# A macaron block with retention and pooling: the inverse roots of the norms go to all partitions by a store to DRAM and a broadcast load instead of by products with diagonal matrices

## The chip, the core and the metric

The kernel runs on one core of one Trainium2 chip. The time is that of the device for one execution, in microseconds, as the median over several executions. The profiled execution is one more of the same program, taken by the hardware profiler; its span runs from its first instruction to its last.

## What is computed

The reference takes x of 1024 tokens by 1024 channels in float32 and runs one layer (cut to what matters):

```python
h = h + 0.5 * swiglu_ffn(rmsnorm(h, norm_ffn1), ffn1_w_in, ffn1_w_out)      # D_FF = 2816
u = rmsnorm(h, norm_mix)
q, k, v, g_ret, p, gates = split(u @ w_in)                                    # 7168 columns
q, k = rotary(q), rotary(k) * 256 ** -0.5                                     # 4 heads of 256
ret = retention(q, k, v)                                                      # chunks of 64, decayed state
ret = ret * rsqrt(mean(ret * ret) + 1e-6) * silu(g_ret)
pool_out = multiscale_pool(p, pool_w, pool_scale)                             # windows 2, 4, 8, 16
merged = sigmoid(gate_0) * (ret @ w_ret_up) + sigmoid(gate_1) * (pool_out @ w_pool_up)
h = h + merged @ w_out
h = h + 0.5 * swiglu_ffn(rmsnorm(h, norm_ffn2), ffn2_w_in, ffn2_w_out)
out = rmsnorm(h, norm_final)
# rmsnorm(x, g) = x * rsqrt(mean(x * x) + 1e-6) * g, over the channels of each token
```

There are four RMS norms: n1 ahead of the first feed-forward part, n2 ahead of the mixing part, n3 ahead of the second feed-forward part, and the final one.

## The kernel before

Activations lie with channels on the 128 partitions and tokens along the free dimension: a tile of 128 by 1024 holds 128 channels of all tokens, a half of it (`half(t, j)`) 512 tokens. Each float32 operand of a product is split into a rounded part (a cast on ScalarE, line 141) and the rest (a subtraction on VectorE, line 142), and each product is three TensorE passes (lines 161 to 163). The large products go by a Strassen-like scheme of seven block products (`strassen`); a group's products are named by their weights, L11, S2, S1, S3, L12, S4, L22, and its banks a, b and e. `ffn_in` computes gate and up of a feed-forward part in 22 groups of 128 columns (`a0`, `a11`, `a1`, ... in the first, `c0`, `c11`, `c1`, ... in the second), `ffn_out` the way back (names with `b` and `d`), `projections` the products of the mixing part.

A norm's factor depends on the token alone, so it is not applied to the operand: the gain per channel goes into the operands, and the factor multiplies the results as they leave PSUM or later. For that the factor must stand on every partition as a row of 1024 numbers, the tile `rb` (`n1rb`, `n2rb`, `n3rb`). `inverse_root` (lines 184 to 207) yields a tile `r` with tokens on the partitions: 128 by 8 for a norm, 128 by 4 or 128 by 2 for a part of the last norm. `token_sums` gets there by products with a column of ones. `spread` (lines 217 to 225) turns `r` into rows: for each group of 128 tokens VectorE multiplies the identity matrix by a column of r (line 223), and one product of a matrix of ones with these diagonals (line 224) puts the row on every partition in a PSUM bank. `Next.stats` does that twice for 512 tokens each and copies both halves to `rb` on ScalarE (line 321).

The final norm comes in three parts of tokens as the last products end (`Last.end`): part 0 is tokens 512 to 1023, part 1 tokens 0 to 255, part 2 tokens 256 to 511. The last product of `ffn_out` is cut the same way: `near` computes the left 256 columns of the four banks `dp6b0` to `dp6b3` for all eleven steps, `far(i)` then the right 256 columns of one bank after the other. As each ends, `part` adds it to the residual (line 721: an eviction `dacc<-dp6b`), squares are summed into `n4ssq` (lines 242 and 243), and when all four are in, the part's sum (`fin0sum`, `fin1sum`, `fin2sum`, line 213), root, factor (`fin0b`, `fin1b`, `fin2b`) and eight scalings (line 1284) follow, each with a store to the output.

All DMAs are issued by SP (`load`, line 129), in one queue, in an order that a scheduler sets with the orders of the other engines when the program is built; instructions of one engine run in that order. A transfer that has to wait holds those behind it. Where a factor's tile exists already when an eviction is written, `ffn_in` uses it there (line 489); otherwise it multiplies later (line 493). Background work is handed out between products by `Flow`; `tc.high_priority` marks evictions.

Of the kernel before, what the change touches and what calls it, by code (L numbers as in the profile page):

```python
# [10 lines left out]
F32 = mybir.dt.float32  # L11
# [6 lines left out]
P = 128  # L18
# [66 lines left out]
def block_kernel(ctx: ExitStack, tc, x, x_tok, vecs, f1_in, f1_out, w_in, pool_w, w_ret, w_pool, w_o,  # L85
                 f2_in, f2_out, rope, decay, consts, out):
    nc = tc.nc
# [4 lines left out]
    copy = nc.scalar.copy  # L92
# [6 lines left out]
    dr = ctx.enter_context(tc.tile_pool(name="dr", bufs=1, space=bass.MemoryType.DRAM))  # L99
# [9 lines left out]
    def raw(name):  # L109
        return sb.tile([P, S], F32, tag="raw", bufs=N_RAW, name=name)  # L110
# [4 lines left out]
    def t4(name):  # L115
        return sb.tile([P, S], F32, tag="t4", bufs=N_T4, name=name)

    def c2(name):
        return sb.tile([P, H], F32, tag="c2", bufs=N_C2, name=name)

    def bank(name):
        return ps.tile([P, H], F32, tag="ps", name=name)
# [5 lines left out]
    def load(dst, src):  # L128
        nc.sync.dma_start(dst, src)
# [4 lines left out]
    def half(t, j):  # L134
        return t[:, j * H : (j + 1) * H]
# [48 lines left out]
    def inverse_root(sums, n, name, by=None):  # L184

        m = sums.shape[-1]

        def st(k):
            return sb.tile([P, 8], F32, tag="st", bufs=10, name=f"{name}{k}")[:, :m]

        v, r0, r1, t = st("v"), st("r0"), st("r1"), st("t")
        if by is None:
            nc.vector.tensor_scalar(v, sums, 1.0 / n, EPS, MUL, ADD)
        else:
            tt(v, sums, by[0], MUL)
            nc.vector.tensor_scalar(v, v, EPS, None, ADD)
        act(r0, v, AF.Sqrt)
        nc.vector.reciprocal(r1, r0)

        tt(t, r1, r1, MUL)  # L200
        tt(t, t, v, MUL)
        nc.vector.tensor_scalar(t, t, -0.5, 1.5, MUL, ADD)
        r = sb.tile([P, 8], F32, tag="rt", bufs=3, name=f"{name}r")[:, :m]
        tt(r, r1, t, MUL)
        if by is not None:
            tt(r, r, by[1], MUL)
        return r

    def token_sums(ssq, tiles, name):

        sums = bank(f"{name}sum")
        for k, j in enumerate(tiles):
            mm(sums[:, k : k + 1], ssq[:, j * P : (j + 1) * P], ones[:, :1], start=k == 0, stop=True,
               skip_group_check=True)
        return sums[:, : len(tiles)]

    def spread(r, name):

        n = r.shape[-1]
        b = bank(f"{name}b")[:, : n * P]  # L220
        dg = c2(f"{name}dg")[:, : n * P]
        for j in range(n):
            nc.vector.tensor_scalar(dg[:, j * P : (j + 1) * P], ident, r[:, j : j + 1], None, MUL)
        mm(b, ones, dg, start=True, stop=True)
        return b

    class Norm:


# [15 lines left out]
    class Next(Norm):  # L245
# [69 lines left out]
        def stats(self, sums=None):  # L315
            def go():
                r = inverse_root(sums if sums is not None else token_sums(self.ssq, range(8), self.name), D, self.name)
                self.r_tok = r
                rb = t4(f"{self.name}rb")
                for q in range(2):  # L320
                    copy(half(rb, q), spread(r[:, 4 * q : 4 * q + 4], f"{self.name}{q}"))
                self.rb = rb

            flow.add(go)
# [434 lines left out]
    ra, rb = raw("ra"), raw("rb")  # L759
# [506 lines left out]
    class Last(Norm):  # L1266
# [6 lines left out]
        def end(self, part):  # L1273
            tokens = (slice(H, S), slice(0, HD), slice(HD, H))[part]
            at = {}

            def stats():
                r = inverse_root(token_sums(self.ssq, range(tokens.start // P, tokens.stop // P), f"fin{part}"), D,
                                 f"fin{part}")
                at["b"] = spread(r, f"fin{part}")  # L1280

            def scale(mt):
                t = self.tiles[mt][:, tokens]
                stt(t, t, vec[:, V_FINAL + mt : V_FINAL + mt + 1], at["b"], MUL, MUL)
                load(out[mt, :, tokens], t)

            flow.add(stats, *(lambda mt=mt: scale(mt) for mt in range(KT)))

    fin = Last("n4")
# [92 lines left out]
```

## Time and profile before

| | |
|---|---|
| median of 3 runs | 2199.36 us (2199.76, 2199.36, 2197.19) |
| profiled execution | 2200.49 us |
| its span | 2198.7 us, 27345 instructions |
| TensorE busy | 2179.3 us, 99% |
| VectorE busy | 1628.7 us, 74% |
| ScalarE busy | 966.6 us, 44% |
| DMA queue of SP | 109152 packets, 308.05 MB, 40.0% of 16 engines' span |
| granted TensorE clock, mean | 0.998 |

Names: PE is the TensorE product and PEld its weight load, DVE is VectorE, ACT is ScalarE, SPq the sequencer of SP that issues the DMAs. A row of a timeline has start and length in us, engine, line, operation, written tile, read tiles, shapes, and in brackets how long the engine was idle before and what ended that. A matmul with float32 operands is recorded as two (x2). In the chain of waits a row is the piece of the span that the chain spends in that work. `x16, 128.0 KB, 1.8` in the list of DMA issues means sixteen transfers of 128 KB, a median of 1.8 us from issue to landing.

### The profile page before, as it was taken

The page shows a single profiled execution, that of the slowest core. Times are in us where ns is not written, and L with a number is a line of the kernel's source. Part 1 is how long each engine was busy: PE and PEld are TensorE (multiplying, and loading weights), DVE is VectorE, ACT ScalarE, POOL GpSimd, SP SyncE. Part 2 cuts the span into 40 slices and gives each one's busy share as a digit, 9 for nine tenths or more (in the row PEclk, how much of TensorE's full clock was granted, in tenths as well). Part 3 has the DMA queues.
Part 4 walks back from the last instruction along what each step waited for, and adds up shares of the span by engine and source line. Part 5 has one row for each costly group of instructions (what it writes and reads, how often), then busy time and mean ns, then how long its engine had stood idle before and what let it go on. Part 6 is the DMA issues. An engine that isn't in the chain of part 4 may idle for free.

```text
span 2198.7 us, 27345 instructions
## 1 busy us (share of the span) xinstructions
PE 2179.3 (99%) x10108; PEld 1818.6 (83%) x10108; DVE 1628.7 (74%) x2682; ACT 966.6 (44%) x1702; POOL 0.2 (0%) x4
## 2 busy tenths in 40 slices
PE   9999999999999999999999999999999999999998
PEld 7888888888888888888888998888888888888887
DVE  8787677887686777686867667775877777788775
ACT  7533333444554434334346554443533333344451
POOL 0000000000000000000000000000000000000000
PEclk9999999999999999999999999999999999999999
DMA  5244232495323323233235465363142323249522
GB/s 210 96 152 150 91 119 97 149 327 185 129 93 119 133 101 128 103 115 115 103 127 201 146 214 202 125 220 125 58 144 101 125 92 114 98 153 331 183 85 77
DMA packets 109287, 309.80 MB, mean 141 GB/s; under 512 B 12257, under 2 KB 14433, under 8 KB 109153
## 3 DMA queue, kind: packets, MB, share of 16 engines
q1 hardware_dynamic: 109152, 308.05, 40.0%
q8 instruction: 79, 1.29, 0.2%
q14 instruction: 56, 0.45, 0.1%
HBM read 218.35 MB, written 89.65 MB: 140 GB/s over the span
## 4 chain that ended last, share of the span: by engine, by line
PE 92%; DVE 3%; DMA 3%; ACT 1%; issue 1%; SPq 0%; DVEq 0%; ACTq 0%
PE c_b L161 3%; PE c_b L163 3%; PE c_b L162 3%; PE a_b L161 2%; PE a_b L162 2%; PE a_b L163 2%; PE c_a L161 2%; PE c_e L163 2%; PE c_a L163 2%; PE c_e L162 2%; PE c_e L161 2%; PE c_a L162 2%; PE a_e L162 2%; PE a_e L163 2%; PE a_e L161 2%; PE a_a L162 2%
## 5 line engine op out<-in xcount | busy, mean ns | idle before, releaser
L141 ACT CAST c_wS<-c_S 128x512 fp32r<-128x512 f32 x88 | 54.7, 622 | 132.3 <-PE c_b L163 76.5
L141 ACT CAST a_wS<-a_S 128x512 fp32r<-128x512 f32 x84 | 52.3, 622 | 106.7 <-PE a_b L163 71.6
L142 DVE TENSOR_TENSOR c_wS<-c_S,c_wS 128x512 fp32r<-128x512 f32 x88 | 60.8, 691 | 24.8 <-ACT c_wS L141 24.2
L142 DVE TENSOR_TENSOR a_wS<-a_S,a_wS 128x512 fp32r<-128x512 f32 x84 | 58.0, 690 | 23.7 <-ACT a_wS L141 23.3
L161 PE MATMUL c_a<-n3R,c_wL 128*128 128x512 f32 x176 | 68.6, 390 | 0.0
L162 PE MATMUL c_b<-n3T,c_wS 128*128 128x512 f32 x176 | 68.5, 389 | 0.0
L161 PE MATMUL c_b<-n3T,c_wS 128*128 128x512 f32 x176 | 68.5, 389 | 0.0
L162 PE MATMUL c_a<-n3R,c_wL 128*128 128x512 f32 x176 | 68.5, 389 | 0.0
L163 PE MATMUL c_a<-n3R,c_wL 128*128 128x512 f32 x176 | 68.5, 389 | 0.0
L163 PE MATMUL c_b<-n3T,c_wS 128*128 128x512 f32 x176 | 68.5, 389 | 0.0
L161 PE MATMUL a_a<-n1R,a_wL 128*128 128x512 f32 x168 | 65.8, 391 | 0.0
L163 PE MATMUL a_a<-n1R,a_wL 128*128 128x512 f32 x168 | 65.4, 389 | 0.0
L162 PE MATMUL a_a<-n1R,a_wL 128*128 128x512 f32 x168 | 65.4, 389 | 0.0
L161 PE MATMUL a_b<-n1T,a_wS 128*128 128x512 f32 x168 | 65.4, 389 | 0.0
L162 PE MATMUL a_b<-n1T,a_wS 128*128 128x512 f32 x168 | 65.4, 389 | 0.0
L163 PE MATMUL a_b<-n1T,a_wS 128*128 128x512 f32 x168 | 65.4, 389 | 0.0
L141 ACT CAST c_wL<-c_ra 128x512 fp32r<-128x512 f32 x44 | 27.3, 621 | 43.4 <-PE c_e L163 38.0
L141 ACT CAST a_wL<-a_ra 128x512 fp32r<-128x512 f32 x42 | 26.0, 621 | 38.0 <-PE a_e L163 38.0
L142 DVE TENSOR_TENSOR c_wL<-c_ra,c_wL 128x512 fp32r<-128x512 f32 x44 | 30.4, 691 | 11.7 <-ACT c_wL L141 11.4
L162 PEld LDWEIGHTS c_b<-n3T,c_wS 128*128 128x128 f32 x176 | 33.0, 188 | 6.9
L162 PEld LDWEIGHTS c_a<-n3R,c_wL 128*128 128x128 f32 x176 | 33.0, 188 | 6.9
L163 PEld LDWEIGHTS c_a<-n3R,c_wL 128*128 128x128 f32 x176 | 33.0, 188 | 6.9
(2369 smaller groups left out, 7225.7 us busy)
## 6 DMA issues: line engine op xcount, KB each, us to landing
c_ra<-in_f_in SPq DMA_DIRECT2D x22, 512.0 KB, 3.6
c_rb<-in_f_in SPq DMA_DIRECT2D x22, 512.0 KB, 5.1
a_ra<-in_f_in SPq DMA_DIRECT2D x21, 512.0 KB, 3.6
a_rb<-in_f_in SPq DMA_DIRECT2D x21, 512.0 KB, 5.2
t<-au SPq DMA_DIRECT2D x11, 512.0 KB, 2.7
b<-an SPq DMA_DIRECT2D x11, 512.0 KB, 3.2
r<-au SPq DMA_DIRECT2D x11, 512.0 KB, 3.8
br<-r SPq DMA_DIRECT2D x11, 512.0 KB, 6.0
```

Source lines behind the costliest of these rows:

```text
L141: copy(hi, src)
L142: tt(lo, src, hi.bitcast(F32), SUB)
L161: mm(dst, w[0], m[0], start=start, stop=False, skip_group_check=True)
L162: mm(dst, w[0], m[1], start=False, stop=False, skip_group_check=True)
L163: mm(dst, w[1], m[0], start=False, stop=stop, skip_group_check=True)
```

## The change

A new function `spread_by_dma` writes the tile r to a line in DRAM, one number per token, and loads that line back to all 128 partitions. The line's store has runs of one number (128 by 8 by 1 for a norm); the load reads the same 4 KB (2 KB for part 0 of the final norm, 1 KB for part 1) once for each partition. The three norms load into `rb`; parts 0 and 1 of the final norm load into a tile in SBUF instead of the PSUM bank. Part 2 of the final norm keeps `spread`.

```diff
--- before.py
+++ after.py
@@ -224,6 +224,14 @@
         mm(b, ones, dg, start=True, stop=True)
         return b
 
+    def spread_by_dma(r, name, dst):
+
+        n = r.shape[-1]
+        line = dr.tile([n, P], F32, tag=f"{name}line", name=f"{name}line")
+        with nc.allow_non_contiguous_dma(reason="one number per token"):
+            load(line.rearrange("j p -> p j"), r)
+        load(dst, line.rearrange("j p -> (j p)").unsqueeze(0).to_broadcast([P, n * P]))
+
     class Norm:
 
 
@@ -317,8 +325,7 @@
                 r = inverse_root(sums if sums is not None else token_sums(self.ssq, range(8), self.name), D, self.name)
                 self.r_tok = r
                 rb = t4(f"{self.name}rb")
-                for q in range(2):
-                    copy(half(rb, q), spread(r[:, 4 * q : 4 * q + 4], f"{self.name}{q}"))
+                spread_by_dma(r, self.name, rb)
                 self.rb = rb
 
             flow.add(go)
@@ -1277,7 +1284,11 @@
             def stats():
                 r = inverse_root(token_sums(self.ssq, range(tokens.start // P, tokens.stop // P), f"fin{part}"), D,
                                  f"fin{part}")
-                at["b"] = spread(r, f"fin{part}")
+                if part == 2:
+                    at["b"] = spread(r, f"fin{part}")
+                else:
+                    at["b"] = c2(f"fin{part}b")[:, : tokens.stop - tokens.start]
+                    spread_by_dma(r, f"fin{part}", at["b"])
 
             def scale(mt):
                 t = self.tiles[mt][:, tokens]
```

On SP's queue each pair stands as line and load: behind n1's line come the two weight loads of group a13, then the load; behind n2's line its load directly, ahead of the stores of v0 and v1; n3's line stands behind group c12's first weight load, the second one comes between line and load; fin0's pair stands ahead of all stores to the output, fin1's between part 0's stores and part 1's. On TensorE fin1sum moves behind 8 products of far(1).

The scheduler also places other work differently; the prediction speaks of three places. VectorE in the third norm, before, from the first use of the factor on (`c0_a` to `c11_b` are PSUM banks of the first two groups of the second feed-forward part, `c1_...` weights of the third):

```order
L489 TENSOR_TENSOR cg0_13283<-c0_a_13117,n3rb_13307 128x512
L489 TENSOR_TENSOR cg11_13344<-c11_a_13155,n3rb_13307 128x512
L489 TENSOR_TENSOR cg0_13283<-c0_b_13149,n3rb_13307 128x512
L142 TENSOR_TENSOR c1_wL11_13401<-c1_ra_13397,c1_wL11_13401 128x512
L142 TENSOR_TENSOR c1_wS3_13433<-c1_S3_13431,c1_wS3_13433 128x512
L489 TENSOR_TENSOR cg11_13344<-c11_b_13168,n3rb_13307 128x512
L347 TENSOR_TENSOR c1_S1_13457<-c1_rb_13398 128x512
L493 TENSOR_TENSOR cu11_13345<-cu11_13345,n3rb_13307 128x512
L347 TENSOR_TENSOR c1_S2_13459<-c1_S1_13457,c1_ra_13397 128x512
L487 TENSOR_TENSOR cu0_13284<-c0_e_13264,c0_v_13193 128x512
L502 TENSOR_TENSOR cu0_13284<-cg0_13283,cu0_13284 128x512
L142 TENSOR_TENSOR c1_wS2_13461<-c1_S2_13459,c1_wS2_13461 128x512
```

Now, beginning with the ninth instruction behind the root n3r:

```order
L142 TENSOR_TENSOR c1_wL11_13362<-c1_ra_13358,c1_wL11_13362 128x512
L142 TENSOR_TENSOR n3T42_13411<-h2_6_12925,n3T42_13411 128x512
L142 TENSOR_TENSOR n3T43_13415<-h2_7_13081,n3T43_13415 128x512
L354 TENSOR_TENSOR c1_S2_13420<-c1_S1_13418,c1_ra_13358 128x512
L142 TENSOR_TENSOR c1_wS3_13394<-c1_S3_13392,c1_wS3_13394 128x512
L496 TENSOR_TENSOR cg0_13257<-c0_a_13091,n3rb_13281 128x512
L496 TENSOR_TENSOR cg0_13257<-c0_b_13123,n3rb_13281 128x512
L496 TENSOR_TENSOR cg11_13305<-c11_a_13129,n3rb_13281 128x512
L496 TENSOR_TENSOR cg11_13305<-c11_b_13142,n3rb_13281 128x512
L142 TENSOR_TENSOR c1_wS2_13422<-c1_S2_13420,c1_wS2_13422 128x512
L500 TENSOR_TENSOR cu0_13258<-cu0_13258,n3rb_13281 128x512
```

The four multiplications by n3rb stand behind the split of the weights c1_wS3 and together ahead of that of c1_wS2; before, wS3 stood between them.

VectorE at the end, part 0 of the final norm, before (from its fifth scaling on):

```order
L1284 SCALAR_TENSOR_TENSOR dacc4_16559<-dacc4_16559,vec_66,fin0b_17926 128x512
L1284 SCALAR_TENSOR_TENSOR dacc5_16561<-dacc5_16561,vec_66,fin0b_17926 128x512
L1284 SCALAR_TENSOR_TENSOR dacc6_16563<-dacc6_16563,vec_66,fin0b_17926 128x512
L1284 SCALAR_TENSOR_TENSOR dacc7_16565<-dacc7_16565,vec_66,fin0b_17926 128x512
L721 SCALAR_TENSOR_TENSOR dacc4_16559<-dp6b0_16391,dacc4_16559 128x256
L721 SCALAR_TENSOR_TENSOR dacc5_16561<-dp6b1_16392,dacc5_16561 128x256
L721 SCALAR_TENSOR_TENSOR dacc6_16563<-dp6b2_16393,dacc6_16563 128x256
L721 SCALAR_TENSOR_TENSOR dacc7_16565<-dp6b3_16394,dacc7_16565 128x256
L243 TENSOR_TENSOR n4ssq_17340<-n4ssq_17340,n4q4_0_18117 128x256
L243 TENSOR_TENSOR n4ssq_17340<-n4ssq_17340,n4q5_0_18120 128x256
L243 TENSOR_TENSOR n4ssq_17340<-n4ssq_17340,n4q6_0_18123 128x256
```

Now:

```order
L1295 SCALAR_TENSOR_TENSOR dacc4_16520<-dacc4_16520,vec_66,fin0b_17887 128x512
L728 SCALAR_TENSOR_TENSOR dacc4_16520<-dp6b0_16352,dacc4_16520 128x256
L728 SCALAR_TENSOR_TENSOR dacc5_16522<-dp6b1_16353,dacc5_16522 128x256
L728 SCALAR_TENSOR_TENSOR dacc6_16524<-dp6b2_16354,dacc6_16524 128x256
L728 SCALAR_TENSOR_TENSOR dacc7_16526<-dp6b3_16355,dacc7_16526 128x256
L1295 SCALAR_TENSOR_TENSOR dacc5_16522<-dacc5_16522,vec_66,fin0b_17887 128x512
L1295 SCALAR_TENSOR_TENSOR dacc6_16524<-dacc6_16524,vec_66,fin0b_17887 128x512
L1295 SCALAR_TENSOR_TENSOR dacc7_16526<-dacc7_16526,vec_66,fin0b_17887 128x512
L251 TENSOR_TENSOR n4ssq_17301<-n4ssq_17301,n4q4_0_18075 128x256
L251 TENSOR_TENSOR n4ssq_17301<-n4ssq_17301,n4q5_0_18078 128x256
L251 TENSOR_TENSOR n4ssq_17301<-n4ssq_17301,n4q6_0_18081 128x256
```

Three of the eight scalings by fin0b stand behind the four evictions of near's banks; five stand ahead of them.

VectorE at the end, part 1, before:

```order
L1284 SCALAR_TENSOR_TENSOR dacc0_16551<-dacc0_16551,vec_66,fin1b_18144 128x256
L1284 SCALAR_TENSOR_TENSOR dacc1_16553<-dacc1_16553,vec_66,fin1b_18144 128x256
L1284 SCALAR_TENSOR_TENSOR dacc2_16555<-dacc2_16555,vec_66,fin1b_18144 128x256
L1284 SCALAR_TENSOR_TENSOR dacc3_16557<-dacc3_16557,vec_66,fin1b_18144 128x256
L721 SCALAR_TENSOR_TENSOR dacc5_16561<-dp6b1_16392,dacc5_16561 128x256
L1284 SCALAR_TENSOR_TENSOR dacc4_16559<-dacc4_16559,vec_66,fin1b_18144 128x256
L1284 SCALAR_TENSOR_TENSOR dacc5_16561<-dacc5_16561,vec_66,fin1b_18144 128x256
L1284 SCALAR_TENSOR_TENSOR dacc6_16563<-dacc6_16563,vec_66,fin1b_18144 128x256
L1284 SCALAR_TENSOR_TENSOR dacc7_16565<-dacc7_16565,vec_66,fin1b_18144 128x256
L243 TENSOR_TENSOR n4ssq_17340<-n4ssq_17340,n4q5_256_18236 128x256
L721 SCALAR_TENSOR_TENSOR dacc6_16563<-dp6b2_16393,dacc6_16563 128x256
L243 TENSOR_TENSOR n4ssq_17340<-n4ssq_17340,n4q6_256_18239 128x256
```

Now:

```order
L1295 SCALAR_TENSOR_TENSOR dacc0_16512<-dacc0_16512,vec_66,fin1b_18102 128x256
L1295 SCALAR_TENSOR_TENSOR dacc1_16514<-dacc1_16514,vec_66,fin1b_18102 128x256
L1295 SCALAR_TENSOR_TENSOR dacc2_16516<-dacc2_16516,vec_66,fin1b_18102 128x256
L1295 SCALAR_TENSOR_TENSOR dacc3_16518<-dacc3_16518,vec_66,fin1b_18102 128x256
L728 SCALAR_TENSOR_TENSOR dacc6_16524<-dp6b2_16354,dacc6_16524 128x256
L1295 SCALAR_TENSOR_TENSOR dacc4_16520<-dacc4_16520,vec_66,fin1b_18102 128x256
L1295 SCALAR_TENSOR_TENSOR dacc5_16522<-dacc5_16522,vec_66,fin1b_18102 128x256
L1295 SCALAR_TENSOR_TENSOR dacc6_16524<-dacc6_16524,vec_66,fin1b_18102 128x256
L1295 SCALAR_TENSOR_TENSOR dacc7_16526<-dacc7_16526,vec_66,fin1b_18102 128x256
L251 TENSOR_TENSOR n4ssq_17301<-n4ssq_17301,n4q6_256_18196 128x256
L728 SCALAR_TENSOR_TENSOR dacc7_16526<-dp6b3_16355,dacc7_16526 128x256
L251 TENSOR_TENSOR n4ssq_17301<-n4ssq_17301,n4q7_256_18233 128x256
```

The eviction of far(1), dp6b1, stands ahead of the scalings by fin1b, and those of far(2) and far(3), dp6b2 and dp6b3, behind four and eight of them.

## The prediction, made before the changed kernel had run

> **What bounds the kernel now.** I read the page first: busy time by engine, and the chain that ended last.
>
> ```profile
> span 2198.7 us, 27345 instructions
> PE 2179.3 (99%) x10108; PEld 1818.6 (83%) x10108; DVE 1628.7 (74%) x2682; ACT 966.6 (44%) x1702; POOL 0.2 (0%) x4
> ...
> PE 92%; DVE 3%; DMA 3%; ACT 1%; issue 1%; SPq 0%; DVEq 0%; ACTq 0%
> ```
>
> TensorE is busy for all but 19 us and is 92% of the chain. Then I asked for busy time in the stretches around three of the places that change (columns: stretch, its length, then busy us and count of PE, PEld, DVE, ACT, POOL, then clock and DMA):
>
> ```profile
> 80.00:100.00 20.00, 20.00 (x86) 15.88 (x85) 15.35 (x32) 10.88 (x17) 0.00 (x0) 1.00 0.12 41
> 1560.00:1600.00 40.00, 40.00 (x181) 32.47 (x180) 36.72 (x70) 22.47 (x38) 0.00 (x0) 1.00 0.26 77
> 2157.00:2187.00 30.00, 29.69 (x241) 28.95 (x240) 17.58 (x49) 3.05 (x9) 0.00 (x0) 1.00 0.29 106
> ```
>
> In all three TensorE has no room: 20.00 of 20.00, 40.00 of 40.00, 29.69 of 30.00 us. Whatever leaves its queue moves the end forward by as much, unless something new makes it wait. VectorE (36.72 of 40) has little room around the third norm. So two questions decide: what do the removed products cost TensorE, and does a factor that now comes by DMA arrive before somebody on TensorE's path needs it?
>
> **What is removed.** The chain of waits, in order of time, has the products that go (start, length, what):
>
> ```profile
> 88.52 0.86 PE n10b L224 x2
> 89.38 0.86 PE n11b L224 x2
> ...
> 674.65 1.12 PE n20b L224 x2
> 675.77 0.86 PE n21b L224 x2
> ...
> 1577.37 0.86 PE n30b L224 x2
> 1578.23 0.86 PE n31b L224 x2
> ...
> 2161.35 0.86 PE fin0b L224 x2
> ...
> 2176.67 0.43 PE fin1b L224 x2
> ```
>
> First norm 0.86 + 0.86 = 1.72, second 1.12 + 0.86 = 1.98 (0.26 of it a wait for its diagonal), third 1.72: 5.42 us. fin0 0.86, fin1 0.43. **Together 6.71 us off the path.** The diagonals on VectorE and ScalarE's six copies into the rb tiles go too; I cost them at nothing, because TensorE covers them in the rows above; without that cover they would be a further gain, not a loss.
>
> **What is added.** Five pairs of DMAs on SP's queue: a store of n numbers per partition, one number per run, and a load of the line to all 128 partitions; SP waits between them. No such store is in the trace. The nearest rows: a store and a load of the same tensor one behind the other (SP's timeline, then the landing times of these two), single transfers by size from the list of issues, the landing of the 128x64 vector load, and all packets of the queue:
>
> ```profile
> 127.38 0.32 SPq L129 DMA_DIRECT2D r<-au  x1
> ...
> 130.04 0.32 SPq L129 DMA_DIRECT2D br<-r  x1
> ...
> DMA to landing us min/median/max: 2.6/2.9/3.2
> ...
> out<-dacc SPq DMA_DIRECT2D x16, 128.0 KB, 1.8
> dec<-in_decay SPq DMA_DIRECT2D x4, 256.0 KB, 3.2
> c_rb<-in_f_in SPq DMA_DIRECT2D x22, 512.0 KB, 5.1
> ...
> DMA to landing us min/median/max: 1.9/1.9/1.9
> ...
> q1 hardware_dynamic: 109152, 308.05, 40.0%
> ```
>
> The pair of 512 KB transfers takes 2.6 (store landed; the load goes out 2.66 after it) + 3.2 = 5.9 us. That is the template. The open term is p, the time of one 4-byte element on its DMA engine. With 16 engines there are 64 elements per engine for a norm (1024 numbers), 32 for fin0, 16 for fin1. Below, p is 0: then the store is no slower than the smallest one, 1.8 us. Above, p is that of an average packet of 2.8 KB: 0.400 x 2198.7 x 16 / 109152 = 129 ns. I take **p = 40 ns**, nearer to nothing: from 128 to 512 KB the rows go from 1.8 to 2.6 us, so time there follows bytes, and an element has 4. Loads: 1.9 (the small vector) to 3.2 us; 3.2 for fin0 (256 KB, as dec), 2.5 between the two for fin1 (128 KB), 5.1 for the norms, whose load goes out among weight loads. SP's turn adds 0.1 (2.66 against 2.6). So from root to factor: fin0 1.8 + 1.3 + 3.2 + 0.1 = 6.4 us (4.4, with a load of 2.5, to 9.2), fin1 1.8 + 0.6 + 2.5 + 0.1 = 5.0 (4.0 to 7.2).
>
> The Trainium skill's page "DMA: Bandwidth & Descriptors", in its section on the anatomy of one DMA, gives a fit of 2.0 us plus bytes over 436 GB/s (for DMAs that GpSimd issues; these come from SP): an estimate from it is 4.6 us for fin0 and 4.3 for fin1, and the sum by that would be the full 6.7.
>
> **Where the factor is needed.** VectorE's timeline: when each root is done and what stands at or just ahead of its first use; then SP's first transfer behind the new pair of the second norm, and TensorE's product that bounds the third norm:
>
> ```profile
> 74.03 0.17 DVE L204 TENSOR_TENSOR n1r<-n1r,n1t 128x8 f32<-128x8 f32 x1
> 86.54 0.69 DVE L142 TENSOR_TENSOR a_wL<-a_ra,a_wL 128x512 fp32r<-128x512 f32 x1
> ...
> 671.37 0.17 DVE L204 TENSOR_TENSOR n2r<-n2r,n2t 128x8 f32<-128x8 f32 x1
> 696.19 0.69 DVE L841 TENSOR_TENSOR p0A<-p0a,n2rb 128x512 f32<-128x512 f32 x1 [0.29 <-PE p0a L163]
> ...
> 1575.22 0.16 DVE L204 TENSOR_TENSOR n3r<-n3r,n3t 128x8 f32<-128x8 f32 x1
> ...
> 677.89 0.33 SPq L129 DMA_DIRECT2D v<-v0A  x1
> ...
> 1597.34 0.39 PE L161 MATMUL c_b<-n3T,c_wS 128*128 128x512 f32 x1
> ```
>
> Norm 1: the first use stands behind the a_wL split, 13 us after the root. Norm 2: 24 us. Norm 3: in the new order 13 VectorE instructions of 0.6 to 0.7 us stand ahead of it, and a late factor first hurts when the split of group c1's S2 weights, which stands behind four multiplications by n3rb, is late for the product at 1597.34 (1595.6 without the removed products): about 17 us after the root. At p = 40 the pair costs 1.8 + 2.6 + 5.1 + 0.2 = 9.7 us: all three are hidden, and the 5.42 us stay. On SP the pair is followed by transfers that waited for something later anyway: the nearest is v0's store, at 677.89, 6.3 us after the root, while SP is held for 1.8 + 2.6 + 0.1 = 4.5. It costs them nothing. If p were so large that 17 us did not do, TensorE would wait there (second rival).
>
> **The end is tighter.** VectorE's timeline there, and fin1's sum from the chain:
>
> ```profile
> 2158.81 0.16 DVE L204 TENSOR_TENSOR fin0r<-fin0r,fin0t 128x4 f32<-128x4 f32 x1
> ...
> 2162.24 5.35 DVE L1284 SCALAR_TENSOR_TENSOR dacc<-dacc,vec,fin0b 128x512 f32<-128x512 f32 x8 [2.36 <-PE fin0b L224]
> 2168.95 1.50 DVE L721 SCALAR_TENSOR_TENSOR dacc<-dp6b,dacc 128x256 f32<-128x256 f32 x4 [1.36 <-PE dp6b L163]
> 2170.38 2.01 DVE L243 TENSOR_TENSOR n4ssq<-n4ssq,n4q 128x256 f32<-128x256 f32 x4
> 2173.99 0.42 DVE L721 SCALAR_TENSOR_TENSOR dacc<-dp6b,dacc 128x256 f32<-128x256 f32 x1 [1.61 <-PE dp6b L163]
> ...
> 2173.95 0.34 PE fin1sum L213 x4
> ...
> 2175.56 0.16 DVE L204 TENSOR_TENSOR fin1r<-fin1r,fin1t 128x2 f32<-128x2 f32 x1
> ...
> 2177.14 1.66 DVE L1284 SCALAR_TENSOR_TENSOR dacc<-dacc,vec,fin1b 128x256 f32<-128x256 f32 x4 [0.57 <-PE fin1b L224]
> ...
> 2186.73 0.42 DVE L721 SCALAR_TENSOR_TENSOR dacc<-dp6b,dacc 128x256 f32<-128x256 f32 x1 [2.56 <-PE dp6b L163]
> ```
>
> I follow the new order on the old clock, with only fin0b's and fin1b's own time taken out. fin0 arrives at 2158.97 + 6.4 = 2165.4. Five scalings at 0.67: 2168.7. Four evictions, 1.5: 2170.2. Three scalings, 2.0: 2172.2. Three sums at 0.50, the eviction of the next product, 0.4, and a sum, 0.5: 2174.6. TensorE now comes to fin1sum at 2173.95 - 0.86 + 8 products at 0.12 = 2174.05, so it waits **0.55 us**. The root follows 1.8 after the sum, at 2176.4; fin1 arrives 5.0 later, at 2181.4. Four scalings 1.66, eviction 0.4, four scalings 1.66, sum 0.4: 2185.5. The last product ends at 2186.73 - 0.86 - 0.43 + 0.55 = 2186.0, later than VectorE is free. So fin1 is hidden by 0.5 us, and the end gains 6.71 - 0.55 = **6.2 us**. At the lower bound of p nothing waits: 6.7. At the upper (9.2 and 7.2 us) fin1sum waits 3.4, fin1 arrives at 2186.4, and VectorE is free for the last eviction only at 2190.5, 3.8 after 2186.73: the gain is 5.42 - 3.8 = 1.6.
>
> The profiled execution took 2200.49 us, 1.8 more than its span, and lies 1.1 above the median of the runs. By the sum its successor has a span of 2192.5; the median goes from 2199.36 to **2193.2**.
>
> **Rivals.** *The end eats the gain.* fin0b holds VectorE's queue with the evictions behind it, then fin1b holds it with the last two. For it: the slack is 0.5 us in all. Each 10 ns of p beyond 40 cost 0.3 to 0.5 us; from about 85 ns the gain falls under 4.4 us, and at 129 it is 1.6, so 2197.8. A slow load (128 readers of one 2 KB line) does the same. Against it: the byte rows above.
>
> *Slower: an element costs more than any average packet.* Runs of 4 bytes, next to those of other engines in memory, are written one after the other. Above 155 ns the third norm is late too (1.8 + 64 p + 5.3 exceeds 17 us), TensorE waits there 64 ns per ns of p, and the end loses 48 ns per ns: 1.6 - 0.048 (p - 129) - 0.064 (p - 155) reaches -4.4 us at p = 197 ns. At 250 ns it is -10.3, so 2209.7. For it: nothing in the trace has so short a run in memory. Against it: it needs more than 1.5 times an average packet's time for a thousandth of its bytes. The skill speaks for this one: the same page's table of specifications says that transfers under 512 B are done by reading, modifying and writing, and its rules for kernel authors that a strided last dimension makes one descriptor per element; it has no price for either, and no run here shows one yet.
>
> **How the numbers follow.** 0.2% is 4.4 us, about what a measurement of this kernel can tell from no change. My forecast (p under 85 ns) 0.62: faster. The eaten gain (85 to 197 ns) 0.26: no change. The slow element 0.12: slower. The forecast's own range is 4.4 to 6.7 us of gain: 2192.7 to 2195.0. The range takes in the upper bound of p and a little beyond it, and the runs' own spread (2197.19 to 2199.76, some 1.3 each way): 2191.4 to 2200.0.
>
> **What will show it.** Between the root and the landing of the load: 6.4 us at fin0, 5.0 at fin1, under 13 at the norms. In TensorE's rows no gap above 0.3 us at the first uses of n1rb, n2rb, n3rb, and one of about 0.5 at fin1sum. VectorE waits for a DMA at fin0b for some 6 us and at fin1b for some 2. Busy time of TensorE falls by 6 to 7 us. A store that lands later than 4 us at fin0, or a wait of TensorE behind n3rb, makes the prediction wrong.

## The result and the profile after

The median goes from 2198.92 us (before, 4 runs, 2197.19 to 2199.76) to 2221.88 us (after, 4 runs, 2221.75 to 2223.93): a ratio of 1.0109, interval 1.0097 to 1.0121. The change makes the kernel 23 us slower, where 6 us less were forecast. The profiled execution took 2223.93 us.

The page of the kernel after, its first lines:

```profile
span 2222.2 us, 27299 instructions
PE 2178.2 (98%) x10092; PEld 1820.4 (82%) x10092; DVE 1621.3 (73%) x2652; ACT 962.3 (43%) x1696; POOL 0.2 (0%) x4
```

The span grew by 23.5 us. TensorE's busy time fell by 1.1 us (2179.3 to 2178.2), not by the 6.7 us that were taken out of its queue. What TensorE waited for, after (who waits, for whom, us in total, times, longest):

```profile
PE fin2sum L213 <- DVE n4ssq L251: 10.0, 1, 10.0
PE dp6b L161 <- DVE dacc L728: 8.4, 1, 8.4
PE c_b L161 <- ACT c_b L384: 6.3, 1, 6.3
...
PE a_b L161 <- ACT a_b L384: 2.2, 1, 2.2
```

and the only one of these that the same view has of the kernel before:

```profile
PE fin2sum L213 <- DVE n4ssq L243: 1.6, 1, 1.6
```

The new waits are 2.2 (first norm) + 6.3 (third norm) + 8.4 (at the end, ahead of far(0)) + 10.0 - 1.6 (at fin2sum) = 25.3 us. With 1.1 us less of work that makes 24.2, against 23.5 in the spans: this is where the time went. The first question is why the factors came so late. The list of DMA issues, after, in the stretches of the first norm, the third, and the end (bytes, then us from issue to landing):

```profile
a_ra<-in_f_in SPq DMA_DIRECT2D x1, 512.0 KB, 14.1
a_rb<-in_f_in SPq DMA_DIRECT2D x1, 512.0 KB, 14.9
n1rb<-n1line SPq DMA_DIRECT2D x1, 512.0 KB, 8.2
n1line<-n1r SPq DMA_DIRECT2D x1, 4.0 KB, 10.6
...
n3line<-n3r SPq DMA_DIRECT2D x1, 4.0 KB, 15.1
...
fin0b<-fin0line SPq DMA_DIRECT2D x1, 256.0 KB, 3.2
fin1b<-fin1line SPq DMA_DIRECT2D x1, 128.0 KB, 4.9
fin0line<-fin0r SPq DMA_DIRECT2D x1, 2.0 KB, 11.5
fin1line<-fin1r SPq DMA_DIRECT2D x1, 1.0 KB, 9.3
```

Every store took 9 to 15 us, and it hardly matters how many numbers it has: 1 KB takes 9.3, 2 KB 11.5, 4 KB 10.6 and 15.1. Of the loads at the end fin0's took the 3.2 us of the forecast, fin1's 4.9 instead of 2.5. Two more things stand there. The two weight loads issued right behind the store of n1 took 14.1 and 14.9 us; before the change they took

```profile
a_ra<-in_f_in SPq DMA_DIRECT2D x1, 512.0 KB, 3.4
a_rb<-in_f_in SPq DMA_DIRECT2D x1, 512.0 KB, 4.1
```

So the store holds up what is behind it, and the load of n1rb, issued when the store has landed, comes out among those weights and takes 8.2 us. And where nothing else is under way, the store's time is not busy time of the DMA engines. Busy time by stretch, after, first while fin0's store was under way (2163.9 to 2175.4), then while n3's store was, with a weight load behind it (the last two numbers are the DMA share and GB/s):

```profile
2165.00:2169.00 4.00, 4.00 (x35) 4.00 (x35) 0.00 (x0) 0.00 (x0) 0.00 (x0) 1.00 0.02 0
...
1584.00:1588.00 4.00, 4.00 (x20) 3.30 (x19) 0.00 (x0) 0.08 (x1) 0.00 (x0) 1.00 0.96 32
```

At fin0 the DMA engines are nearly idle (0.02), and VectorE does nothing: it waits. At the third norm they count as busy (0.96) while only 32 GB/s move. What takes the time inside the store is not shown. VectorE's timeline, after, first uses of the four factors (in brackets the idle time and what ended it):

```profile
91.44 0.69 DVE L500 TENSOR_TENSOR ag<-ag,n1rb 128x512 f32<-128x512 f32 x1 [5.43 <-DMA n1rb<-n1line]
...
1594.29 0.69 DVE L496 TENSOR_TENSOR cg<-c_a,n3rb 128x512 f32<-128x512 f32 x1 [11.91 <-DMA n3rb<-n3line]
...
2178.59 3.40 DVE L1295 SCALAR_TENSOR_TENSOR dacc<-dacc,vec,fin0b 128x512 f32<-128x512 f32 x5 [14.77 <-DMA fin0b<-fin0line]
...
2206.11 1.67 DVE L1295 SCALAR_TENSOR_TENSOR dacc<-dacc,vec,fin1b 128x256 f32<-128x256 f32 x4 [11.23 <-DMA fin1b<-fin1line]
```

At the end the lateness reaches TensorE through the evictions. TensorE's row with the wait of 8.4 us is the first product of far(0):

```profile
2182.38 0.58 PE L161 MATMUL dp6b<-dp4m,dp4w 128*128 128x256 f32 x1 [8.39 <-DVE dacc L728]
```

It writes the right half of the bank dp6b0, whose left half VectorE has to evict first. On VectorE that eviction stands behind the five scalings by fin0b: it begins at 2181.91 and takes 0.42 us. fin1sum comes 41 products later and waits for nothing.

At the norms TensorE does not wait for VectorE itself. Its releaser is line 384 on ScalarE, the copy of bank a into bank b that opens a group's sum. ScalarE's timeline, after, at the first norm and at the third:

```profile
93.37 1.06 ACT L506 ACTIVATE ag<-ag 128x1024 f32<-128x1024 f32 x1 [3.63 <-DVE ag L500]
94.33 0.58 ACT L384 COPY a_b<-a_a 128x512 f32<-128x512 f32 x1
...
1595.66 1.28 ACT L506 ACT_TABLE_LOAD   x1 [11.58 <-DVE cg L496]
...
1599.89 0.57 ACT L384 COPY c_b<-c_a 128x512 f32<-128x512 f32 x1
```

The swish of a group (line 506, the activation of its gate) needs values that VectorE has multiplied by the factor, stands ahead of that copy in ScalarE's queue, and so passes the lateness on. The last question is the 5.6 us by which TensorE's busy time fell too little. Busy time by stretch for TensorE alone, after (stretch, length, busy, then granted clock), behind the waits at the first norm, the third norm and ahead of far(0):

```profile
97.00:98.00 1.00, 1.00 (x4) 0.50 0.00 0
...
1600.00:1603.00 3.00, 2.48 (x6) 0.50 0.03 5
...
2184.00:2186.00 2.00, 2.00 (x12) 0.50 0.57 219
```

Behind these waits the granted clock (as a share of full speed) was 0.50 for 3.4, 3.4 and 5.2 us of products; at the norms one came every 0.43 us instead of every 0.23. Half of these 12.0 us is extra: 6.0, against the 5.6 looked for.

### The profile page after: what moved, and what is told of

Same layout as the page of the kernel before. It is cut to its first block, busy times and chain, and to the rows that moved or that the text cites. A ratio compares the mean times of both kernels' runs of the same rounds, so it can differ in the third digit from the quotient of the medians.

```text
span 2222.2 us, 27299 instructions
## 1 busy us (share of the span) xinstructions
PE 2178.2 (98%) x10092; PEld 1820.4 (82%) x10092; DVE 1621.3 (73%) x2652; ACT 962.3 (43%) x1696; POOL 0.2 (0%) x4
## 3 DMA queue, kind: packets, MB, share of 16 engines
q8 instruction: 79, 1.29, 0.3%
## 4 chain that ended last, share of the span: by engine, by line
PE 91%; DMA 4%; DVE 3%; ACT 1%; issue 1%; SPq 0%; DVEq 0%; ACTq 0%
PE c_b L161 3%; PE c_b L162 3%; PE c_b L163 3%; PE a_b L161 2%; PE a_b L163 2%; PE a_b L162 2%; PE c_e L161 2%; PE c_a L161 2%; PE c_e L163 2%; PE c_a L163 2%; PE c_e L162 2%; PE c_a L162 2%; PE a_e L163 2%; PE a_e L162 2%; PE a_e L161 2%; PE a_a L163 1%
## 5 line engine op out<-in xcount | busy, mean ns | idle before, releaser
L161 PEld LDWEIGHTS c_b<-n3T,c_wS 128*128 128x128 f32 x176 | 33.4, 190 | 13.6 <-ACT c_b L384 6.7
L161 PEld LDWEIGHTS a_b<-n1T,a_wS 128*128 128x128 f32 x168 | 32.0, 190 | 10.0 <-ACT a_b L384 2.7
L163 PEld LDWEIGHTS c_b<-n3T,c_wS 128*128 128x128 f32 x176 | 33.5, 190 | 7.0
L162 PEld LDWEIGHTS c_b<-n3T,c_wS 128*128 128x128 f32 x176 | 33.5, 190 | 7.0
```

Source lines behind the costliest of these rows:

```text
L161: mm(dst, w[0], m[0], start=start, stop=False, skip_group_check=True)
L162: mm(dst, w[0], m[1], start=False, stop=False, skip_group_check=True)
L163: mm(dst, w[1], m[0], start=False, stop=stop, skip_group_check=True)
```

## The experiments

Three theories at the start. **A**: the price is the form of the store, 4-byte numbers side by side in memory, and not their count. **Rivals**: any run below some length is slow (B); the number of runs is what counts (C). Later ones are named where they come up.

### What a small store takes

Run **e1_probes**: sixteen unread stores were added to the kernel before, from 742 to 1131 us (`pr_adj8x` is one of 8 numbers per partition, `P` is 128):

```diff
+            if what == "adj":
+                load(d(n, P).rearrange("j p -> p j"), src[:, :n])
+            elif what == "gap":
+                load(d(8, P, n // 4).rearrange("j p w -> p j w")[:, :, 0], src[:, :8])
+            elif what == "one":
+                load(d(1, P, n // 4).rearrange("j p w -> p j w")[:, :, 0], src[:, :1])
+            elif what == "run":
+                load(d(P, n // 4), src[:, : n // 4])
...
+                probe(t["c"])
```

> The kernel before, with sixteen small stores that nobody reads added in the projections, each from a tile that VectorE has just written; only their time from issue to landing is looked at, not the kernel's. Names: adj is one number per token, numbers of neighbouring tokens next to each other in DRAM, 8, 2 or 1 per partition (adj8 is the store of a norm, adj2 that of fin1); gap64 and gap512 are the 1024 numbers of adj8, each alone in 64 or 512 bytes of DRAM; one512 is 128 numbers, each alone in 512 bytes; run32 to run512 are one run of that many bytes per partition; rows8 is 8 rows of 512 bytes. Theory A (short writes into the same stretch of DRAM are acknowledged one after the other): adj8, adj2 and adj1 all land after 8 to 12 us, because the stretches have as many writers in all three; gap512, gap64 and one512 land within 3 to 4 us. Theory B (any run below some length is acknowledged late, whatever lies beside it): adj, gap and one512 all take 8 to 12 us, run32 too, and there is a length from run64 to run512 at which it falls to 2 to 3 us. Theory C (the number of runs): adj8 10 us, adj2 4, adj1 and one512 3, gap64 and gap512 as adj8. In all three run512 and rows8 take 2 to 3 us.

The list of DMA issues of this kernel:

```profile
pr_adj8x<-q0c SPq DMA_DIRECT2D x1, 4.0 KB, 11.8
pr_run32x<-q0c SPq DMA_DIRECT2D x1, 4.0 KB, 7.4
...
pr_gap64y<-k2c SPq DMA_DIRECT2D x1, 4.0 KB, 2.5
pr_run32y<-k2c SPq DMA_DIRECT2D x1, 4.0 KB, 1.4
pr_one512x<-q3c SPq DMA_DIRECT2D x1, 0.5 KB, 1.4
...
pr_adj1y<-k3c SPq DMA_DIRECT2D x1, 0.5 KB, 8.1
```

The same 128 numbers land in 1.4 us when each stands alone, 512 B from the next, and in 8.1 when they stand side by side. The same 1024 numbers take 2.5 with 64 B from one to the next and 11.8 side by side; as 128 runs of 32 B they take 1.4. B falls (runs of 32 and of 4 bytes at 1.4), C falls (1024 runs at 2.5, 128 at 8.1), A holds. The first 32-byte store was issued 7.9 us behind a side-by-side one that was still under way, and took 7.4 instead of 1.4: here too the slow store holds the next.

Run **e7_probes**, a second set, asked how the price grows as numbers come closer, and whether neighbours must come from different partitions (`own8`: 8 numbers of one partition in 64 B that hold no other's):

```diff
+            elif what == "own":
+                load(d(P, 16).rearrange("p (j w) -> p j w", w=2)[:, :, 0], src[:, :8])
...
+    probes = iter("run8x gap8x run16x adj8z gap32x gap16x one512y own8x rows8y adj4x run16y gap8y "
+                  "gap32y gap16y run8y own8y".split())
```

> The kernel before with sixteen small stores of 128 partitions that nobody reads. adj: 4-byte numbers side by side in memory from neighbouring partitions (16 writers per 64 B); gap8, gap16, gap32: 8 numbers per partition, the neighbours' numbers 8, 16, 32 bytes apart (8, 4, 2 writers per 64 B); run8, run16: one run of 8 or 16 bytes per partition, without gaps (8, 4 writers per 64 B); own8: 8 numbers of one partition 8 bytes apart in the same 64 B, with no other partition in it; rows8: 8 rows of 512 B; one512: one number per partition, 512 B apart. Theory A (each further writer of the same 64 B costs some 0.45 to 0.55 us): adj8 10 to 12 us, adj4 9 to 10, gap8 6.6, gap16 4.5, gap32 3.4, run8 4.6, run16 2.8, rows8 and one512 1.4 to 1.6; own8 1.4 to 2 if writers have to be different partitions, 4.6 to 6 if any eight writes into one 64 B count. Rival D (any number that stands nearer than 64 B to another is read, modified and written at one price): gap8, gap16, gap32 all land in 8 to 11 us like adj.

```profile
pr_run8x<-q0c SPq DMA_DIRECT2D x1, 1.0 KB, 2.9
pr_gap8x<-q0c SPq DMA_DIRECT2D x1, 4.0 KB, 4.5
...
pr_adj8z<-k0c SPq DMA_DIRECT2D x1, 4.0 KB, 11.0
pr_gap32x<-q1c SPq DMA_DIRECT2D x1, 4.0 KB, 2.8
pr_gap16x<-q1c SPq DMA_DIRECT2D x1, 4.0 KB, 3.6
...
pr_own8x<-k1c SPq DMA_DIRECT2D x1, 4.0 KB, 6.3
```

For 1024 numbers: 2.8 us at 32 B apart, 3.6 at 16, 4.5 at 8 (5.4 the second time), 11.0 at 4. The rival of one price for all close numbers falls. But theory A's law of 0.45 to 0.55 us per writer of the same 64 B was wrong too: it gave 6.6 us for 8 writers, and runs of 8 B, also 8 writers, took 2.9 and not 4.6. The price rises slowly down to 8 B and then about doubles. Neighbours from different partitions are not needed (6.3 for one partition's own). What in the memory or in the acknowledging does this is not settled; that the numbers lie densely is what the runs show. The store of rows of 512 B and two others have no landing time in the records.

### One place at a time

Run **e2_norms_dma**: the norms by DMA, the last norm as before.

```diff
-                for q in range(2):
-                    copy(half(rb, q), spread(r[:, 4 * q : 4 * q + 4], f"{self.name}{q}"))
+                spread_by_dma(r, self.name, rb)
```

> The change at the three norms alone; parts 0 and 1 of the last norm by products as before. If the places add up as the shifts of TensorE's rows in the two traces read (first norm +2.6 us, second -2.0, third +5.9), the time is 2199 + 6 = 2205 us, with TensorE waiting some 2 us behind n1rb and 6 behind n3rb. If the loss came from the end alone and the norms were hidden, as predicted, it is 2199 - 5 = 2194.

2202.31 us against 2198.07: ratio 1.002 (1.001 to 1.0029). The other way round, **e3_fin_dma**: the last norm's two parts by DMA and the three norms as before.

```diff
-                at["b"] = spread(r, f"fin{part}")
+                if part == 2:
+                    at["b"] = spread(r, f"fin{part}")
+                else:
+                    at["b"] = c2(f"fin{part}b")[:, : tokens.stop - tokens.start]
+                    spread_by_dma(r, f"fin{part}", at["b"])
```

> The change at parts 0 and 1 of the last norm alone; the norms by products as before. If the places add up (fin0 +10 to 11 us, fin1 +8 to 9), the time is 2199 + 19 = 2218 us, with some 8.5 us of wait at fin1sum and 10 at fin2sum. If one of the two waits covers the other, it is under 2212.

2214.12 us: ratio 1.0077 (1.006 to 1.0094). The losses, 4.2 and 16.1 us, add up to 20.3 of the 23; the end is the larger part, and the 2.7 us left over are no more than the intervals allow. Both runs came out below what the shifts in the traces had given (2205 and 2218). In the second TensorE waits 6.9 us ahead of far(0) and 8.4 at fin2sum, and not at fin1sum. The norms by themselves, worth 5.4 us by the sum, cost 4.2.

### The store in another form

**e4_rows, turned rows.** One TensorE product turns the 128 by 8 roots into 8 rows of 128, ScalarE copies them, and the store writes rows of 512 B:

```diff
-        with nc.allow_non_contiguous_dma(reason="one number per token"):
-            load(line.rearrange("j p -> p j"), r)
+        b = bank(f"{name}turn")
+        row = sb.tile([8, P], F32, tag="row", bufs=2, name=f"{name}row")[:n]
+        nc.tensor.transpose(b[:n, :P], r, ident)
+        copy(row, b[:n, :P])
+        load(line, row)
```

> The changed kernel with only the form of the store altered: r is turned by one TensorE transpose and copied out of PSUM by ScalarE, so that the store writes n rows of 512 bytes instead of 128 n numbers; line and load are the same. If the short runs are what made it slow, the stores land within 2 to 3 us instead of 9 to 15, factor and root lie 5 to 8 us apart, the waits of TensorE at n1 and n3 go, and the time is what the prediction said less the turns: 2193 to 2197 us. If the store is late for another reason (a store and a load in a row on SP's queue, memory just written being read back), the stores still take over 8 us and the time stays above 2215.

2191.89 us (2190.74 to 2195.24): ratio 0.9974 (0.9964 to 0.9984), faster than both kernels and than the 2193 to 2197 expected. SP issues the load 1.1 to 1.2 us behind the store at the first norm and at both parts of the end, and 2.6 behind it at the other two norms. VectorE's timeline at the end:

```profile
2158.89 2.74 DVE L1298 SCALAR_TENSOR_TENSOR dacc<-dacc,vec,fin0b 128x512 f32<-128x512 f32 x4 [6.57 <-DMA fin0b<-fin0line]
...
2174.60 0.48 DVE L1298 SCALAR_TENSOR_TENSOR dacc<-dacc,vec,fin1b 128x256 f32<-128x256 f32 x1 [1.81 <-DMA fin1b<-fin1line]
```

The four waits of TensorE are gone. But this run changed two things, since the scheduler set another order behind the turn. ScalarE's timeline at the first norm:

```profile
90.93 0.57 ACT L387 COPY a_b<-a_a 128x512 f32<-128x512 f32 x1 [1.62 <-PE a_a L163]
...
97.49 1.28 ACT L509 ACT_TABLE_LOAD   x1
```

The copy now stands ahead of the swish. VectorE gets n1rb at 93.69 here, later than in the kernel after (91.44), because the turn stands far back in TensorE's queue, and still TensorE does not wait. So was it the order (rival O) or the store? Two runs ask that.

**e8_turn_back, the same turn and the old store.** The turned row is turned back, and stored as in the kernel after:

```diff
-        load(line, row)
+        nc.tensor.transpose(b[:, P : P + n], row, ident[:n, :n])
+        back = sb.tile([P, 8], F32, tag="back", bufs=2, name=f"{name}back")[:, :n]
+        copy(back, b[:, P : P + n])
+        with nc.allow_non_contiguous_dma(reason="one number per token"):
+            load(line.rearrange("j p -> p j"), back)
```

> e4_rows with one step more: the row of 512 B runs that TensorE's turn gives is turned back by a second TensorE product, copied by ScalarE, and stored as in the kernel after, one 4-byte number per run. The place of the spreading among the other work, and the order of the engines around it, stay nearly e4's (on VectorE 87 lines of difference in some 2580 rows); the form of the store is what differs, with some 1 to 2 us for the second turn. Theory A (the form of the store costs 8 to 15 us): n1line, n2line, n3line, fin0line and fin1line land in 8 to 15 us instead of 1.2 to 2.6; VectorE waits over 5 us for n1rb, n3rb, fin0b and fin1b, TensorE stalls, most of all at fin1sum and fin2sum, and the time goes from e4's 2191.9 to 2208 to 2226. Rival O (what e4 gained came from the other order of the engines that the turn brought, not from the store): 2192 to 2197.

2225.24 us: ratio 1.0124 (1.0109 to 1.0139). Its DMA issues at the first norm and at the end:

```profile
n1line<-n1back SPq DMA_DIRECT2D x1, 4.0 KB, 8.7
...
fin0line<-fin0back SPq DMA_DIRECT2D x1, 2.0 KB, 10.1
fin1line<-fin1back SPq DMA_DIRECT2D x1, 1.0 KB, 8.2
```

TensorE waits again: 7.2 us at the first norm, 8.4 ahead of far(0), 9.7 at fin2sum. There are 33 us between two kernels that differ in the form of the store, in a second turn (it puts the first norm's store off by 2.0 us, from 88.8 to 90.8), and in what the scheduler moved for it: the form is the cause, and the turn's order does not help by itself.

**e5_pmajor, no turn, runs of 32, 16 and 8 bytes.** The line is kept with one partition's numbers side by side; VectorE then reads the factor with a stride. The order of VectorE and ScalarE at the first norm is that of the kernel after:

```diff
-        line = dr.tile([n, P], F32, tag=f"{name}line", name=f"{name}line")
-        with nc.allow_non_contiguous_dma(reason="one number per token"):
-            load(line.rearrange("j p -> p j"), r)
-        load(dst, line.rearrange("j p -> (j p)").unsqueeze(0).to_broadcast([P, n * P]))
+        line = dr.tile([P, n], F32, tag=f"{name}line", name=f"{name}line")
+        load(line, r)
+        load(dst, line.rearrange("p j -> (p j)").unsqueeze(0).to_broadcast([P, n * P]))
...
+        rb = rb.rearrange("c (p j) -> c j p", p=P)[:, js, :]
+        tt(by_group(dst), by_group(src), rb, MUL)
```

> The kernel after, but the line is kept with the numbers of one partition side by side (128 by 8 instead of 8 by 128), so that the store writes one run of 32 B per partition for a norm (16 B for fin0, 8 B for fin1) and no 4-byte runs; the factor's tile then holds group 0..7 of a token row side by side, and VectorE reads it with a stride of 8 (4, 2) numbers. Nothing is added on TensorE. The order of VectorE and ScalarE at the first norm is the same as in the kernel after, row by row. Theory A (writes beside each other in one 64 B of memory are acknowledged one after the other, some 0.45 us per writer): norm stores land in 1.4 to 2.0 us, fin0's (4 writers per 64 B) in 2.8, fin1's (8 writers) in 4.6; no TensorE gap above 0.3 us at n1 and n3; fin0 at 6 to 7.6 us from its root, fin1 at 9.4, so the end loses 1 to 5 of the 6.7 us; time 2192 to 2197. Rival O (what the turned rows gained at the norms came from their other order of the engines, not from the store): the gap of 2.4 us at n1 and that of 6.3 at n3 stay; time 2198 to 2204. Rival S (VectorE reads the strided factor slower): multiplications by n1rb and n3rb take more than the 0.69 us of 128x512, at twice that some 100 us more of VectorE's time, and stalls of TensorE in every group.

2205.71 us: ratio 1.0035 (1.0021 to 1.0048). The time that theory A gave (2192 to 2197) was missed, but its part on the store holds in the unchanged order. The first norm's issues:

```profile
a_rb<-in_f_in SPq DMA_DIRECT2D x1, 512.0 KB, 4.1
n1rb<-n1line SPq DMA_DIRECT2D x1, 512.0 KB, 4.9
n1line<-n1r SPq DMA_DIRECT2D x1, 4.0 KB, 1.4
```

The weights behind the store are back at 4.1 us, fin0's store (16 B runs) took 1.4 and fin1's (8 B runs) 4.3, and TensorE no longer waits at the two products of the first and third norm where it waited 2.2 and 6.3 us. The time that this won went to rival S. VectorE's groups, this kernel:

```profile
L239 DVE TENSOR_TENSOR au<-au,n1rb 128x512 f32<-128x512 f32 x44 | 50.1, 1144 | 0.0
```

A multiplication by the strided factor takes 1144 ns instead of 0.69 us. VectorE's busy time is 99 us above that of the kernel after (1720.5), and TensorE waits in other places: 3.0 us for a_v and 1.9 for a later a_b in the first groups, 1.1 each ahead of far(0) and at fin1sum, 3.3 at fin2sum. That the slower multiplications cause these waits is argued from the rows, not tested.

**e9_rows_norms, turned rows at the norms alone**, the last norm by products as before:

```diff
-                if part == 2:
-                    at["b"] = spread(r, f"fin{part}")
-                else:
-                    at["b"] = c2(f"fin{part}b")[:, : tokens.stop - tokens.start]
-                    spread_by_dma(r, f"fin{part}", at["b"])
+                at["b"] = spread(r, f"fin{part}")
```

> e4's turned rows at the three norms, products with diagonals for the last norm as in the kernel before. If each part of the prediction's sum holds once the store is fast, the norms give 5.42 us less the three turns (some 0.1 to 0.2 each): 2198.1 - 5.0 = 2193, and the last norm in e4 gave the other 1.2. If VectorE's waits for fin0b and fin1b in e4 (6.6 and 1.8 us) ate what the last norm's products cost, this kernel is as fast as e4, 2191 to 2192.

2191.09 us (2190.92 to 2193.32): ratio 0.997 (0.9959 to 0.9982). It is as fast as with the last norm by DMA, the intervals overlap. So the DMAs at the end win nothing that can be told even with the fast store, and what there is to win is in the norms.

### Who holds whom at the first norm

Run **e6_swish_behind**: to the norms by DMA (e2) one edge was added, so that the first swish stands behind the copy a_b<-a_a on ScalarE.

```diff
+                nx.first_sum = copy(t["b"], t["a"])
...
+                        with tc.issue_after(nx.first_sum.ins):
+                            act(gate, gate, AF.Silu)
```

> The norms by DMA as in e2_norms_dma, fin by products; the one difference is that on ScalarE's queue the first swish of the first feed-forward part (which waits for the multiplications by n1rb) is made to stand behind the copy a_b<-a_a that TensorE waits for, instead of ahead of it. VectorE's rows keep their order, the factor is as late as before. Theory Q (TensorE stalled at n1 because the swish held ScalarE's queue with that copy behind it): the gap at 92.8 us (1.04 in e2, 2.40 in the kernel after) falls under 0.3 though VectorE still waits 4 to 5 us for n1rb; with the products that ran at half clock behind it the time falls by 1 to 3 us against e2's 2202.3. Rival V (the queue of VectorE, held by the late factor, is what TensorE waited for): the gap stays at 1 us or more, only with another instruction as its releaser, and the time stays.

2203.32 us against 2202.31 without the edge: no gain. TensorE's rows with a wait at this norm, first without the edge (`e2`), then with it (`e6`):

```profile
94.03 0.50 PE L161 MATMUL a_b<-n1T,a_wS 128*128 128x512 f32 x1 [0.88 <-ACT a_b L384]
101.59 0.50 PE L161 MATMUL a_b<-n1T,a_wS 128*128 128x512 f32 x1 [1.80 <-ACT a_v L389]
```

```profile
102.50 0.50 PE L164 MATMUL a_b<-n1T,a_wS 128*128 128x512 f32 x1 [3.34 <-ACT a_v L392]
```

The wait for a_b is gone, as theory Q said, and one comes later, for the copy into a_v, which stands behind two more swishes and a cast; the first of these swishes (3.3 us) and the cast (0.8) wait for VectorE. 0.88 + 1.80 became 3.34. ScalarE's queue decides where TensorE waits. That it waits at all is, by the rows, VectorE's backlog of multiplications by a factor for which VectorE itself sat idle for 4.8 us. Theory Q falls as an explanation of the time. Of V the unchanged time and the other releaser came true; the gap did not stay at its place.

## Why the prediction was wrong, step by step

**What was removed: right.** 6.71 us of products left TensorE's queue; with turned rows in their place its busy time is 6.4 us lower than before (2172.9). Turned rows win 6.2 us in all, and 7.2 with the norms alone, on intervals 4 to 5 us wide. That 6.2 is also the forecast is partly luck: it is not made of the forecast's parts.

**The price of the store: the step that failed.** The prediction took 1.8 us + p per element per engine, p between 0 and 129 ns; at its 40 ns that is 3.1 us for fin0's store, 2.4 for fin1's and 4.4 for a norm's. The measured times do not go with the count (9.3 us for 256 numbers, 11.5 for 512, 10.6 for 1024), and at fin0 the engines are nearly idle meanwhile. No single p fits: solved for it, fin1's store gives 469 ns, fin0's 303 and n1's 138. For fin1 even the upper bound (1.8 + 16 x 0.129 = 3.9 us) was less than half of 9.3. The bounds came from the packets of other transfers, which say nothing of a form that no transfer in the trace had. The form was in the text, as the third rival's first words (runs of 4 bytes, next to those of others in memory), with a chance of 0.12 and with a price per element that made it need 197 ns. That rival had the direction right, but neither its "others" (one partition's own numbers cost 6.3 us) nor its price by the count.

What the page "DMA: Bandwidth & Descriptors" of the Trainium skill says in its section on the anatomy of one DMA, 2.0 us plus bytes over 436 GB/s (for DMAs that GpSimd issues), holds no better: it gives 2.0 us for a store measured at 7.9 to 15.1. The same page of the Trainium skill warns against a strided last dimension, in its rules for kernel authors, and that pointed the right way. What its table of specifications says of transfers under 512 B does not tell the two apart, since 32-byte runs landed in 1.4 us.

**The end: that price, and a wait in another place.** The root of fin0 is done at 2163.8 and VectorE starts with fin0b at 2178.6: 14.8 us instead of 6.4. The prediction's chain lets TensorE run on to fin1sum, and with 8.4 us more would have it wait 0.55 + 8.4 = 8.95 us there. 8.4 were measured, but ahead of far(0): the chain leaves out that far(0) needs the bank that the eviction behind fin0b frees. The two numbers are alike because neither place had slack. On the forecast's clock that eviction ends at some 2169.2 (2165.4 + 5 x 0.67 + 0.4) and near at some 2169.0 (2173.8 - 0.86 - 33 products at 0.12), both estimates from rows of before. So the missing step cost nothing at the forecast's price, and would have cost as soon as the store was later. fin1 took 14.3 instead of 5.0, 9.3 later, of which 0.5 were hidden: 8.8, and the wait at fin2sum grew by 8.4. With turned rows the lateness is near what the prediction had, 6.6 us at fin0 (6.4) and 4.6 at fin1 (5.0), but by luck: at fin0 it is 2.0 until the turned row is stored, 1.2 for the store and 3.4 for the load, where the prediction had 3.1 for the store and 3.2 for the load. The gain at the end that it drew from this, 1.29 less 0.55, is too small for the two runs with turned rows to show.

**The norms: hidden, it said; two of three were not.** The second norm cost no wait, as forecast. At the first the factor came 18.9 us after its root (72.5 to 91.4), past the 13 us that the prediction gave it, and TensorE waited 2.2. At the third it came 19.9 us after it (1574.4 to 1594.3), the prediction's 17 would have meant a wait of 2.9, and 6.3 were measured: the bound there was not VectorE's split, done at 1597.4, but the copy on ScalarE behind the swish, done at 1600.5, a queue that the prediction did not follow. In the kernel with 32-byte runs, where n3's store took 3.3 us, that wait is gone.

**"It costs them nothing" of the transfers behind the pair: incomplete.** At the second norm v0's store went out at 683.6 and TensorE waited for nothing, as forecast. The prediction did not ask about transfers between store and load. At the first norm the weights there took 11 us longer. Nobody waited for them, but the load of n1rb, taken at 5.1, had to come out among them: 8.2.

**The rest that a wait costs: missing.** The sum counted a wait at its length. The waits at the first and third norm and ahead of far(0) were each followed by products at half the granted clock. By the stretches that is some 6.0 us, and it accounts for the 5.6 us between the work that left the queue (6.7) and the fall of the busy time (1.1). No run took it away by itself.

**The list of what would show it wrong** was right: a store later than 4 us at fin0 (11.5), and a wait of TensorE behind n3rb (6.3).

## What to carry to other kernels

A store that puts 4-byte numbers of many partitions side by side in memory takes 8 to 15 us for 128 to 1024 numbers, and holds the transfers behind it; turn it into rows first, by one small product. Numbers 32 B apart landed in 2.8 us as a store, but loading them back was not tried. Where a form of transfer has no row in the trace, its price has no bound from other rows: measure it by itself with a few unread stores before summing. To see whether a late factor is hidden, follow each queue that it passes (here VectorE's and then ScalarE's) to the instruction that TensorE waits for, and ask which bank a held eviction keeps.

## What the runs showed of the hardware that was not expected

**Dense small writes.** Issue to landing of 1024 numbers by their distance in memory: 11.0 to 11.8 us at 4 B, 4.5 to 5.4 at 8, 3.6 at 16, 2.8 at 32, 2.5 to 3.2 at 64; 1.4 for the same bytes as 32-byte runs (1.4 to 3.3 at the norms of e5_pmajor). 128 numbers side by side still take 8.1.

**The clock behind a short wait.** A wait of 2.2 us (first norm, after) was followed by a granted clock of 0.50, and so was one of 1.80 (norms by DMA, TensorE's stretches):

```profile
103.00:105.00 2.00, 2.00 (x7) 0.50 0.01 4
```

while one of 1.88 us in e5_pmajor and one of 3.34 us (swish behind the copy) were not:

```profile
104.00:106.00 2.00, 2.00 (x10) 1.00 0.01 4
```

The Trainium skill's page "TensorE: Matmul & The Clock Gate", in the section on why this matters for your kernels, asks for no gap above some 3 us; here a shorter one was enough and a longer one went free. The same page says in Part 1 that the activity is watched in windows of 3.4 us that run freely, by which the place of a gap in them would count. The runs agree with that in so far as the length alone does not decide, but none tests it.
